# gr, za and the values of the linear-attention branch as 2x2 block products in seven multiplications

## The chip, the cores and the metric

The kernel runs on one core of a Trainium2 chip. The metric is the device time of one execution in microseconds (us). PE is TensorE (matmuls), ACT is ScalarE, DVE is VectorE, POOL is GpSimd, and SP is the engine from which most DMAs are issued.

## What is computed

One block of a hybrid network on x of 512 tokens by 1024 features, all in float32:

```python
n = rmsnorm(x, g_mix)
gq, gk, gv, gr, z_gf, z_gb, cq, ckv, kr, z_ma, z_mb = split(n @ w_in)   # 1024 x 5824
y_gla  = rmsnorm(gated_linear_attention(gq, gk, gv, z_gf, z_gb), g_gla) * silu(gr)   # 4 heads, values 256 wide
y_mla  = latent_attention(cq, ckv, kr)                                   # 8 heads, values 128 wide
merged = sigmoid(z_ma) * y_gla + sigmoid(z_mb) * y_mla
h = x + merged @ w_out
h = h + square(relu(rmsnorm(h, g_mlp) @ w_ff1)) @ w_ff2                  # 4096 wide
out = rmsnorm(h, g_final)
```

gr, za (that is z_ma) and gv are each 512 tokens by 1024 columns of `n @ w_in`, zb (z_mb) too; gq and gk are 512 by 512, 128 columns for each of the four heads of the linear attention. The scale of the first rmsnorm is one number per token, so the kernel multiplies x (times g_mix) by the weights first and puts the token's scale on the product.

## The kernel before

**Precision.** Both operands of a product are split into hi and lo parts in TensorE's float32r type. `split` (L92 to L94) writes hi on ACT as a rounded copy and lo on DVE as the difference; `split_scaled` (L96 to L98) does it with a factor. `mm3` (L87 to L90) issues three matmuls for each product: hi by hi, hi by lo, lo by hi. Most of the matmuls of the kernel stand at L88, L89 and L90 for that reason.

**Buffers.** SBUF tiles come from pools by size: `u2` (128x512, 25 buffers), `u4` (128x1024, 26), `wf` for weights that have just landed (3), `wh` and `wl` for their halves (128x1024, 4 each). PSUM has two groups of four banks, `mm` and `at`. A tile's buffer goes to a later tile when all its users are done.

**Order.** The framework (Tile) plans the order of the instructions of each engine ahead of time: by the order in which they are traced, by when they are ready in its plan, and by which buffers are free. Where the kernel writes an order out, it uses `in_program_order` (all of a stretch, for some engines) and `goes_behind` (one stretch behind another). At run time every engine works through its own queue in order.

**Stages.** In the opening (L289 to L351), x arrives transposed (features on partitions) in eight pieces, along with eight pieces of the value weights of the first 512 columns. Each piece is split, PE multiplies it at once (`values_with`, L312 to L319, 96 matmuls at L317), and x's squares are summed up to give each token's scale: `r_x` as one number per token on a partition, `R` as a 128x512 tile in which every partition holds the scales of all tokens. `z_chunk` then projects the gates and the rotary key part. After that each projection is one call of `proj_T` (L240): it loads 1024x128 weights, splits them, and PE makes a tile of 128 features by 512 tokens with 24 matmuls of 512 columns. So gr, za, zb, gq and gk have features on partitions, and the token's scale is applied with `R`. `gla_g1` (L539) makes gr's and za's gates for a head; `gla_v` (L505) makes the second half of the values with tokens on partitions.

**Heads.** For each head h of four (L800 to L861): `gla_g1`, then `gla_qk` (gq and gk projected, multiplied by the decays of `gate_parts` on DVE, scaled for neighbouring and far chunks on POOL, L450), a zb projection, `gla_scores`, a second zb projection, `gate_parts` for the next head, and `gla_out` (L556): two 128x512 tiles of features by tokens, 24 matmuls of 512 columns. Its norm over 256 features runs across partitions, so `gla_rstd` sums the squares with matmuls against ones (L255) and `gla_norm` spreads the scale over the partitions with two more (L282). Head 3 also holds the latent projections. Then come the latent attention (L864 to L880), `w_out`, and the squared-ReLU stage.

**The squared-ReLU stage.** The second of its products (`@ w_ff2`) is already done as 2x2 block products in seven multiplications (L1007 to L1090): the weights' block sums (`add_w2`, L997) and the sums of the activations (L1066 to L1069) are made on DVE, and the weights of each product are split two products ahead (`prep`).

Of the kernel before, what the change touches and what calls it, by code (L numbers as in the profile page):

```python
# [56 lines left out]
def tile_block(ctx: ExitStack, tc: tile.TileContext, t, out: bass.AP):  # L57
# [10 lines left out]
    def u2(name, dt=F32, shape=(P, S)):  # L68
        return tl(list(shape), dt, "u2", 25, name)
# [218 lines left out]

    xT = [u4(f"xT{k}") for k in range(KD)]  # L289
# [3 lines left out]
    for k in range(KD):  # L293
        nc.sync.dma_start(xraw[k], t["xt"][k * P : (k + 1) * P, :])
        nc.sync.dma_start(vraw[k], w_in[k * P : (k + 1) * P, C_GV : C_GV + S])
    load_gates()

    def v_tiles(pr):
        return [u4(f"gv{pr}{i}") for i in range(NT)]

    def v_evict(acc, hl, i):
        split_scaled(hl[:, 0, :], hl[:, 1, :], acc, r_x[:, i : i + 1])
# [5 lines left out]
    v_accs = [ps("mm", f"gv0{i}") for i in range(NT)]  # L308
    vh = [halves(2, S, f"gv0{k}") for k in range(KD // 2)]
    sq = None  # L310

    def values_with(k):  # L312
        hi, lo = xT[k][:, 0, :], xT[k][:, 1, :]
        wh, wl = vh[k // 2][0][:, k % 2, :], vh[k // 2][1][:, k % 2, :]
        for x, (a, b) in enumerate(((hi, wh), (hi, wl), (lo, wh))):
            for i in range(NT):
                nc.tensor.matmul(  # L317
                    v_accs[i], a[:, i * P : (i + 1) * P], b, start=k == 0 and x == 0, stop=k == KD - 1 and x == 2
                )  # L319
# [8 lines left out]
    for k in range(KD):  # L328
# [8 lines left out]
        if k < 6:  # L337
            values_with(k)
# [4 lines left out]
    values_with(6)  # L343
    values_with(7)
# [3 lines left out]
    v = v_tiles(0)  # L348
    for i in range(NT):
        v_evict(v_accs[i], v[i], i)  # L350
# [39 lines left out]
    def gate_parts(h):  # L390
        l = u4("l", F32)
        ms = []
        for i, d in enumerate(("f", "b")):
            bcol = (V_BF if d == "f" else V_BB) + h
            bias = gvec[:, bcol : bcol + 1]
            acc = ps("at", f"gate{d}")
# [32 lines left out]

    def gla_qk(h, parts):  # L430
# [3 lines left out]
        for x, (col, name) in enumerate(((C_GQ, "gq"), (C_GK, "gk"))):  # L434
            acc = proj_T(col + h * P, f"{name}{h}")
            n = u2(f"{name}n{h}")
            if x == 0:
                nc.vector.scalar_tensor_tensor(n, acc, GQ_SCALE, R, op0=ALU.mult, op1=ALU.mult)
            else:
                nc.vector.tensor_tensor(n, acc, R, op=ALU.mult)  # L440
            for d in ("f", "b"):
                nc.vector.tensor_tensor(  # L442
                    near[d][:, x].rearrange("p a b -> p (a b)"), n,
                    parts[d][0][:, x].rearrange("p a b -> p (a b)"), op=ALU.mult,
                )
# [59 lines left out]
    def gla_v(pr):  # L505

        accs = [ps("mm", f"gv{pr}{i}") for i in range(NT)]
        col = C_GV + pr * S
        res = v_tiles(pr)

        def piece(i, k2, wh, wl):
            tok = slice(i * P, (i + 1) * P)
            for kk in range(2):
                k = 2 * k2 + kk
                mm3(accs[i], xT[k][:, 0, tok], xT[k][:, 1, tok], wh[:, kk, :], wl[:, kk, :], k == 0, k == KD - 1)

        kept = []
        for k2 in range(KD // 2):
            wh, wl = weights(w_in[k2 * 2 * P : (k2 + 1) * 2 * P, col : col + S], f"gv{pr}{k2}")
            if k2 >= 2:  # L520
                kept.append((k2, wh, wl))
                continue
            for i in range(NT):
                piece(i, k2, wh, wl)
        for i in range(NT):
            for k2, wh, wl in kept:
                piece(i, k2, wh, wl)
            v_evict(accs[i], res[i], i)
        return res

    def gated(acc, name):

        z = u2(f"z{name}")
        nc.vector.tensor_tensor(z, acc, R, op=ALU.mult)  # L534
        th = u2(f"t{name}")
        nc.scalar.activation(th, z, AF.Tanh, scale=0.5)
        return z, th

    def gla_g1(h, js=(0, 1)):  # L539

        res = []
        for j in js:
            f = 2 * h + j
            z, th = gated(proj_T(C_GR + f * P, f"gr{f}"), f"r{f}")
            g1 = u2(f"g1{f}")
            nc.vector.scalar_tensor_tensor(g1, th, 1.0, z, op0=ALU.add, op1=ALU.mult)
            _, ta = gated(proj_T(C_ZA + f * P, f"za{f}"), f"a{f}")
            nc.vector.scalar_tensor_tensor(g1, ta, 1.0, g1, op0=ALU.add, op1=ALU.mult)
            res.append(g1)
        return res  # L550
# [5 lines left out]
    def gla_out(h, sc, v, g1, name):  # L556
        accs = [ps("at", f"{name}o{j}") for j in range(2)]
        for dv in range(2):
            for j in range(NT):
                at = (h % 2) * GDV + dv * P  # L560
                c = slice(at, at + P)
                mm3(accs[dv], v[j][:, 0, c], v[j][:, 1, c], sc[j][:, 0, :], sc[j][:, 1, :],
                    j == 0, j == NT - 1)
        sq = []
        for dv in range(2):
            s = u2(f"{name}sq{dv}")
            nc.scalar.activation(s, accs[dv], AF.Square)
            sq.append(s)
            f = 2 * h + dv
            nc.vector.scalar_tensor_tensor(  # L570
                g1[dv], accs[dv], gla_gain[:, f : f + 1], g1[dv], op0=ALU.mult, op1=ALU.mult
            )
        nc.vector.tensor_tensor(sq[0], sq[0], sq[1], op=ALU.add)
        return sq[0]

    def gla_rstd(sq, g1, name, early):

        at = traced()
        tot = feature_sums(sq, name, "mm")
        if early is not None:  # L580
            goes_behind((at, traced()), early, PE_ONLY)
        return rstd_diag(tot, GDV, name, False), g1, name

    def gla_norm(diag, g1, name):
        rs = spread(diag, name, "mm")
        for dv in range(2):
            nc.vector.tensor_tensor(g1[dv], g1[dv], rs, op=ALU.mult)
        return g1
# [205 lines left out]
    y1, g2 = [], []  # L794
    z_chunk()
    g1 = gla_g1(0, (0,))
    parts = gate_parts(0)
    g1 += gla_g1(0, (1,))
    waiting = None
    for h in range(GH):  # L800
        last = h == GH - 1
        if h:
            g1 = gla_g1(h)
        if h == GH - 2:
            cos, sin = rotary_tables()
        near, nxt, far = gla_qk(h, parts)
        if last:
# [8 lines left out]
            waiting = gla_rstd(*waiting, (marks[1], marks[2]))  # L816
            marks.append(traced())
            next(cq_steps)
            goes_behind((marks[1], marks[2]), (marks[0], marks[1]), PE_ONLY)
            goes_behind((marks[3], traced()), (marks[2], marks[3]), PE_ONLY)  # L820
            ckv = next(ckv_steps)
            y1 += gla_norm(*waiting)
            next(cq_steps)
        if h == 2:
            v = gla_v(1)
        if h == 2:
            began = traced()
            sc = gla_scores(near, nxt, far)
            waiting = gla_rstd(*waiting, (began, traced()))
            g2.append(mla_g2(2 * h))  # L830
        else:
            began = traced()
            zb = proj_T(C_ZB + 2 * h * P, f"zb{2 * h}")
            projected = traced()
            sc = gla_scores(near, nxt, far)
            scored = traced()
            goes_behind((projected, scored), (began, projected), PE_ONLY)
            if h == 1:
# [390 lines left out]
```

## Time and profile before

| what | value |
|---|---|
| time, three runs | 780.64 us median (780.55 to 781.74) |
| profiled execution | 781.0 us, of which span 779.3 us |
| granted TensorE clock, mean | 0.997 |
| busy in the span | PE 770.3 us (99%), DVE 543.8 (70%), ACT 407.1 (52%), POOL 97.8 (13%) |
| instructions | 9996, of which 3728 matmuls |
| DMA | 73.94 MB, 95 GB/s in the mean |

The span goes from the first to the last instruction of the profiled execution; the time of the same execution is 1.7 us longer. Busy shares are means over stages that differ. A matmul's busy time overlaps with the next one's, so its price is read from the distance between starts.

### The profile page before, as it was taken

To read this page: it belongs to the slowest core of one execution; us is meant where nothing else is said; L and a number is where in the kernel's file an instruction comes from. 1 tells how busy PE (TensorE), PEld (TensorE's weight loads), DVE (VectorE), ACT (ScalarE), POOL (GpSimd) and SP (SyncE) were. 2 spreads that over 40 slices of the span, in tenths; PEclk is the share of its full clock that TensorE was granted. 3 is DMA by queue.
4 is the path that set the end of the run, shared out by engine and by line. 5 is a ranking of instruction groups with operands and counts; after the bars stand their busy time and mean duration, and the time that the engine had idled before them with its cause. 6 is when DMAs were issued, how large, how long until landed. Compare 5 with 4: busy or idle time off the path is not lost.

```text
span 779.3 us, 9996 instructions
## 1 busy us (share of the span) xinstructions
PE 770.3 (99%) x3728; PEld 647.9 (83%) x3728; DVE 543.8 (70%) x833; ACT 407.1 (52%) x677; POOL 97.8 (13%) x166
## 2 busy tenths in 40 slices
PE   9999999999999999999999999999999999999996
PEld 7888888888888888898888888888888888888885
DVE  7767555765574459699963578865787578848695
ACT  7463622732462336697852466535554465436644
POOL 1023103203011213221110100000000000000014
PEclk9999999999999999999999999999999999999998
DMA  7633143243323312233033731164106411560002
GB/s 250 178 94 108 27 108 82 61 115 82 82 54 101 56 42 63 53 108 95 28 136 92 261 108 54 56 191 133 54 14 201 141 51 28 163 187 2 28 1 108
DMA packets 102401, 73.94 MB, mean 95 GB/s; under 512 B 15088, under 2 KB 86768, under 8 KB 102352
## 3 DMA queue, kind: packets, MB, share of 16 engines
q1 hardware_dynamic: 101264, 70.14, 31.5%
q10 hardware_dynamic: 864, 2.38, 0.8%
q0 software_dynamic: 224, 0.79, 0.4%
q8 instruction: 29, 0.48, 0.3%
q14 instruction: 20, 0.16, 0.1%
HBM read 69.62 MB, written 2.10 MB: 92 GB/s over the span
## 4 chain that ended last, share of the span: by engine, by line
PE 91%; issue 4%; DVE 2%; POOL 1%; ACT 0%; POOLq 0%
PE f L89 8%; PE f L90 7%; PE f L88 7%; PE gx L88 4%; PE gx L90 4%; PE gx L89 4%; PE gv L317 3%; PE wo L88 2%; PE wo L89 2%; PE gz L89 2%; PE wo L90 2%; PE gr L88 2%; PE za L88 2%; PE za L89 2%; PE gr L89 2%
## 5 line engine op out<-in xcount | busy, mean ns | idle before, releaser
L997 DVE TENSOR_TENSOR w<-w,w 128x1024 f32<-128x1024 f32 x32 | 38.7, 1219 | 0.4
L1172 POOL DMA_DIRECT2D gfin<-in_g_final x1 | 0.7, 653 | 282.7 <-PE f L90 282.7
L759 ACT ACTIVATE e<-s,top 128x512 f32<-128x512 f32 x32 | 21.9, 685 | 5.8 <-DVE top L756 5.8
L944 DVE TENSOR_TENSOR h<-gx,h 128x512 f32<-128x512 f32 x32 | 21.5, 683 | 1.9 <-PE gx L90 1.8
L94 DVE TENSOR_TENSOR pT<-tp,pT 128x512 fp32r<-128x512 f32 x32 | 21.6, 677 | 0.4 <-ACT pT L93 0.4
L756 DVE TENSOR_REDUCE top<-s 128x1 f32<-128x512 f32 x32 | 21.5, 676 | 0.0
L93 ACT ACTIVATE pT<-tp 128x512 fp32r<-128x512 f32 x32 | 18.9, 592 | 3.4 <-PE tp L773 3.3
L773 PE MATMUL tp<-ident,e 128*128 128x128 f32 x128 | 19.2, 272 | 0.0
L88 PE MATMUL av<-pT,v 128*128 128x256 f32 x64 | 19.1, 299 | 0.0
L1050 ACT ACTIVATE fa<-f 128x512 f32<-128x512 f32 x32 | 18.5, 577 | 0.0
L89 PE MATMUL av<-pT,v 128*128 128x256 f32 x64 | 18.4, 287 | 0.0
L90 PE MATMUL av<-pT,v 128*128 128x256 f32 x64 | 18.3, 286 | 0.0
L773 PEld LDWEIGHTS tp<-ident,e 128*128 128x128 f32 x128 | 15.6, 140 | 3.1
L450 POOL TENSOR_TENSOR qk<-qkf,e3f 128x256 f32<-128x256 f32 x8 | 7.9, 981 | 81.8 <-DVE qkf L442 81.8
L791 POOL TENSOR_TENSOR tb<-tb,g 128x512 f32<-128x512 f32 x8 | 11.1, 1382 | 53.1 <-DVE tb L790 40.1
L93 ACT ACTIVATE gbh<-y 128x512 fp32r<-128x512 f32 x16 | 10.1, 634 | 14.0 <-DVE y L1067 14.0
L1059 ACT ACTIVATE px<-fa 128x256 f32<-128x256 f32 x32 | 13.4, 419 | 1.0
L88 PE MATMUL s<-kbuf,q 96*128 96x512 f32 x32 | 13.8, 432 | 0.0
L534 DVE TENSOR_TENSOR za<-za,R 128x512 f32<-128x512 f32 x8 | 5.5, 689 | 11.8 <-PE za L90 11.8
L93 ACT ACTIVATE b_10h<-w 128x1024 fp32r<-128x1024 f32 x7 | 7.4, 1059 | 12.1 <-PE gz L90 6.0
L93 ACT ACTIVATE b_20h<-w 128x1024 fp32r<-128x1024 f32 x7 | 7.4, 1059 | 12.1 <-PE gz L90 6.0
L93 ACT ACTIVATE b_00h<-w 128x1024 fp32r<-128x1024 f32 x7 | 7.4, 1058 | 12.1 <-PE gz L90 6.0
(1454 smaller groups left out, 2791.8 us busy)
## 6 DMA issues: line engine op xcount, KB each, us to landing
w<-in_w_ff SPq DMA_DIRECT2D x64, 256.0 KB, 3.5
x<-in_xt SPq DMA_DIRECT2D x8, 256.0 KB, 5.2
vw<-in_w_in SPq DMA_DIRECT2D x8, 256.0 KB, 5.3
h<-in_x ACTq DMA_DIRECT2D x4, 512.0 KB, 5.2
out<-ms SPq DMA_DIRECT2D x7, 256.0 KB, 2.2
q<-ro SPq DMA_DIRECT2D x16, 64.0 KB, 2.3
gr0f<-in_w_in SPq DMA_DIRECT2D x1, 512.0 KB, 4.9
za0f<-in_w_in SPq DMA_DIRECT2D x1, 512.0 KB, 5.9
```

The costliest lines, as they stand in the source:

```text
L88: nc.tensor.matmul(acc, lh, rh, start=start, stop=False, skip_group_check=onto)
L89: nc.tensor.matmul(acc, lh, rl, start=False, stop=False, skip_group_check=onto)
L90: nc.tensor.matmul(acc, ll, rh, start=False, stop=stop, skip_group_check=onto)
L93: nc.scalar.activation(hi, src, AF.Copy)
L94: rest.tensor_tensor(lo, src, raw(hi), op=ALU.subtract)
L317: nc.tensor.matmul(v_accs[i], a[:, i * P : (i + 1) * P], b, start=k == 0 and x == 0, stop=k == KD - 1 and x == 2)
L756: nc.vector.tensor_reduce(top, acc, axis=AX.X, op=ALU.max, negate=True)
L759: nc.scalar.activation(e, acc, AF.Exp, bias=top, accum_out=tot)
L773: nc.tensor.transpose(tp[:, k * P : (k + 1) * P], e[:, k * P : (k + 1) * P], ident)
L944: nc.vector.tensor_tensor(hc, acc, hc, op=ALU.add)
L997: nc.vector.tensor_tensor(wq[dst][g], wq[x][g], wq[y][g], op=op)
L1050: nc.scalar.activation(a, acc, AF.Relu)
```

## The change

gr, za and gv (each 512 tokens by 1024 columns, over 1024 features) become block products with tokens on partitions. x is cut into four blocks (256 tokens by 512 features), the weights into four blocks (512 by 512), and seven products of blocks, of 24 matmuls each, give the four blocks of the result (Winograd's form). The block sums of x are made once on POOL (`x_sums`, `more_x_sums`) and used by all three; the differences of weight blocks are made on POOL in place (`less`). PE's order over the products, and POOL's from `x_sums` to the last of them, are written out with `in_program_order`. The opening now multiplies gq and gk of head 0 and the first two zb projections with features on partitions (weights in a gathered input, `w_first`); those projections drop out of their later places. The head outputs are made with tokens on partitions (48 matmuls of 256 columns); their norm sums along the row on ACT, the gates are multiplied on DVE, the scale on POOL, and `gla_turn` transposes the result with eight 128x128 transposes a head. The column sums and the spreading of the scale on PE drop out. `u2` has 29 buffers instead of 25, and the DMA scratch space is set to 8192.

```diff
+    def x_sums():
+        add = nc.gpsimd.tensor_tensor
+        for p in range(KD // 2):
+            a, b = xraw[p], xraw[p + KD // 2]
+            for u, k in ((a, p), (b, p + KD // 2)):
+                nc.scalar.activation(u, u, AF.Copy, scale=gmix[:, k : k + 1])
+            y = u2(f"xy{p}")
+            add(y[:, LO], a[:, HI], b[:, HI], op=ALU.add)
+            add(y[:, HI], y[:, LO], a[:, LO], op=ALU.subtract)
+            sy = u4(f"xsy{p}")
+            split(sy[:, 0], sy[:, 1], y)
...
+    class Seven:
+        def load(self, x):
+            self.blocks[x] = [u4(f"{self.name}w{x}{g}", F32, (P, 2, S)) for g in range(2)]
...
+        def less(self, dst, x, y):
+            for g in range(2):
+                nc.gpsimd.tensor_tensor(
+                    self.blocks[dst][g], self.blocks[x][g], self.blocks[y][g], op=ALU.subtract
+                )
+        def prepare(self, m):
+            x = {1: 0, 2: 2, 5: 0, 6: 0, 3: 3, 7: 1, 4: 2}[m]
+            if m == 5:
+                self.less(0, 1, 0)
+            elif m == 6:
+                self.less(0, 3, 0)
+            elif m == 3:
+                self.less(2, 2, 0)
+            elif m == 7:
+                self.less(1, 3, 1)
+            self.right[m] = []
+            for g in range(2):
+                wh, wl = halves(2, S, f"{self.name}{m}{g}")
+                split(wh, wl, self.blocks[x][g])
+                self.right[m].append((wh, wl))
+        def product(self, m):
...
+            for rb in range(2):
+                acc, tok = accs[rb], slice(rb * P, (rb + 1) * P)
+                for p in range(KD // 2):
+                    lh, ll = x_left[p][m]
+                    wh, wl = right[p // 2]
+                    mm3(acc, lh[:, tok], ll[:, tok], wh[:, p % 2, :], wl[:, p % 2, :],
+                        begin and p == 0, p == KD // 2 - 1, not begin)
+                if m in (1, 5, 6):
+                    c = {1: self.c11, 5: self.c22, 6: self.c12}[m][rb]
+                    nc.scalar.activation(c, acc, AF.Copy)
+                elif m == 4:
+                    self.sink(2 + rb, 0, acc, u2(f"{self.name}d"))
+                else:
+                    c = {2: self.c11, 3: self.c12, 7: self.c22}[m][rb]
+                    nc.vector.tensor_tensor(c, acc, c, op=ALU.add)
+                    self.sink(rb + (2 if m == 7 else 0), int(m != 2), c, c)
+    def gr_rows(i, half, src, dst):
+        th = u2(f"tr{i}{half}")
+        nc.scalar.activation(th, src, AF.Tanh, scale=r_half[:, i : i + 1])
+        nc.vector.scalar_tensor_tensor(dst, th, 1.0, src, op0=ALU.add, op1=ALU.mult)
...
     z_chunk()
-    g1 = gla_g1(0, (0,))
...
+    for x in (0, 2, 1, 3):
+        sevens[0].load(x)
+    x_sums()
+    zb_gate(2)
+    steps = [(a, m) for a in range(3) for m in SEVEN]      # order: 1, 2, 5, 6, 3, 7, 4
+    for a, m in steps[:2]: sevens[a].prepare(m)
+    for n, (a, m) in enumerate(steps):
+        if n + 2 < len(steps):
+            b, mm = steps[n + 2]
+            if a + 1 < 3:
+                for x in {3: (0,), 7: (2, 1), 4: (3,)}.get(m, ()): sevens[a + 1].load(x)
+        if m == 7:
+            sevens[a].product(m)
+            if a == 0: zb_gate(3)
+            elif a == 2: project_qk(1, 0)
+        if n + 2 < len(steps):
+            sevens[b].prepare(mm)
+            if n == 0: more_x_sums()
+        if m != 7: sevens[a].product(m)
+        if a == 2 and m == 3: parts = gate_parts(0, "mm")
+    near, nxt, far = gla_qk(0, parts)
     for h in range(GH):
...
+        sc = gla_scores(near, nxt, far)
+        if h:
+            gla_turn(h - 1, (projected, scored))
...
+            project_qk(h + 1, 1)
+            parts = gate_parts(h + 1)
+            gla_out(h, sc)
+            if h < 2: zb_gate(4 + h)
+            if h < 2: project_qk(h + 2, 0)
+            near, nxt, far = gla_qk(h + 1, parts)
```

More of the change, by code (lines that the diff above doesn't have):

```diff
@@ L433, in gla_qk @@
             near[d] = u4(f"qk{d}", F32, (P, 2, NT, P))
[L434 to L440, printed above, removed]
+        for x in range(2):
+            n = qk.pop((h, x))
             for d in ("f", "b"):
@@ L531, in gated @@
[L531 to L550, printed above, removed]
+    SEVEN = (1, 2, 5, 6, 3, 7, 4)
@@ L552, in mla_g2, with gv_rows @@
+    def gv_rows(i, half, src, dst):
+        v[i, half] = u4(f"gv{half}{i}")
+        split_scaled(v[i, half][:, 0, :], v[i, half][:, 1, :], src, r_x[:, i : i + 1])
     def mla_g2(f):
         return gated(proj_T(C_ZB + f * P, f"zb{f}"), f"b{f}")[1]
[L556 to L574 removed]
@@ new lines, in gla_turn @@
+    def gla_turn(h, early=None):
+        half, at = h // 2, (h % 2) * GDV
+        began = traced()
+        for dv in range(2):
+            f = 2 * h + dv
+            tp = ps("at", f"y1{f}")
+            for i in range(NT):
+                nc.tensor.transpose(
+                    tp[:, i * P : (i + 1) * P], g1[i, half][:, at + dv * P : at + (dv + 1) * P], ident
+                )
+            y = u2(f"y1{f}")
+            nc.scalar.activation(y, tp, AF.Copy, scale=gla_gain[:, f : f + 1])
+            y1.append(y)
+        if early is not None:
+            goes_behind((began, traced()), early, PE_ONLY)
```

236 lines of the change are left out of this document (144 added, 92 removed).

## The prediction, made before the changed kernel ran

> **What bounds the kernel now.** I read the page first (busy time, the chain that ended last), then the stretch from 29 to 300 us, in which all the projections lie, then single matmuls for their spacing, and last the vector engines, on which the change puts its new work.
>
> ```profile
> PE 770.3 (99%) x3728; PEld 647.9 (83%) x3728; DVE 543.8 (70%) x833; ACT 407.1 (52%) x677; POOL 97.8 (13%) x166
> ...
> PE 91%; issue 4%; DVE 2%; POOL 1%; ACT 0%; POOLq 0%
> ```
>
> PE is busy for 770.3 of 779.3 us, and the chain is PE for 91%. The windows say the same of the changed stretch (PE, PEld, DVE, ACT, POOL busy, then the granted clock):
>
> ```profile
> 29.00:300.00 271.00, 270.87 (x1262) 226.20 (x1262) 168.60 (x267) 122.47 (x170) 52.36 (x101) 1.00 0.31 79
> ```
>
> PE stands still for 0.13 us of 271; DVE works 62%, ACT 45%, POOL 19%. Every matmul taken away is therefore time won, as long as the others keep up. Busy time per matmul overlaps, so the price is the distance between starts, from the timeline of PE (start, duration):
>
> ```profile
> 45.16 0.39 PE L89 MATMUL gr<-xT,gr1h 128*128 128x512 f32 x1
> 45.39 0.39 PE L90 MATMUL gr<-xT,gr1l 128*128 128x512 f32 x1
> ...
> 396.96 0.28 PE L88 MATMUL av<-pT,v 128*128 128x256 f32 x1
> 397.08 0.28 PE L89 MATMUL av<-pT,v 128*128 128x256 f32 x1
> ```
>
> From 44.71 to 49.47 us lie 21 steps of 512 columns: 0.2267 us each. Steps of 256 columns take 0.119 (396.01 to 397.20, ten of them). The other prices on PE stand in the chain in order of time:
>
> ```profile
> 129.85 0.79 PE gla0ss L255 x8
> 136.70 0.46 PE gla0rs L282 x2
> 436.28 0.87 PE mb L197 x8
> ```
>
> A head's column sums cost 0.79, the spreading of its scale 0.46, eight 128x128 transposes 0.87.
>
> **PE's own sum.** Each of gr, za and values needs 8 x 8 x 3 = 192 matmuls of 512 columns now, and 7 products x 2 x 4 x 3 = 168 after: 3 x 24 x 0.2267 = 16.3 us off. The opening 96 matmuls stay 96 (gq0, gk0, zb0, zb1 instead of values) and the later projections lose just those. Head outputs: 24 x 0.2267 = 5.44 becomes 48 x 0.119 = 5.71, four times: +1.1. Transposes: 4 x 0.87 = +3.5. Column sums and spreading go: 4 x (0.79 + 0.46) = -5.0. Together -16.7 us, all of it on the path, since PE is the path.
>
> **What the rest must now do.** A product takes PE 24 x 0.2267 = 5.44 us. For it ACT and DVE split two 128x1024 blocks, and four products in seven first need two POOL subtractions of 128x1024. DVE and POOL hinder each other, as two timelines side by side show:
>
> ```profile
> 62.33 0.99 POOL L450 TENSOR_TENSOR qk<-qkf,e3f 128x256 f32<-128x256 f32 x1 [5.33 <-DVE qkf L442]
> 63.28 1.59 POOL L450 TENSOR_TENSOR qk<-qkf,c3f 128x256 f32<-128x256 f32 x1
> 64.83 0.61 POOL L450 TENSOR_TENSOR qk<-qkb,e3b 128x256 f32<-128x256 f32 x1
> 757.41 1.29 POOL L1100 TENSOR_TENSOR ms<-h,gfin 128x512 f32<-128x512 f32 x1
> ```
> ```profile
> 62.76 1.64 DVE L94 TENSOR_TENSOR gr2l<-gr2f,gr2h 128x1024 fp32r<-128x1024 f32 x1
> ...
> 757.20 0.68 DVE L944 TENSOR_TENSOR h<-gz,h 128x512 f32<-128x512 f32 x1
> 757.80 1.99 DVE L94 TENSOR_TENSOR b_31l<-w,b_31h 128x1024 fp32r<-128x1024 f32 x1
> ```
>
> The split's subtraction, two SBUF inputs, takes 1.22 us when alone (1.14 between starts). At 757.80 it takes 1.99: it ends 1.1 after POOL's 1.29 us are over. At 62.76 it waits for one POOL instruction (1.64), and POOL's next waits for it (1.59 instead of 0.61). They take turns, whole instructions at a time. The addition at 757.20 reads PSUM and SBUF and isn't lengthened. [...]
>
> POOL's price for 128x1024 is in no row. The nearest stand in its groups of instructions (last: us in all, mean ns of one) and in the answer for line 1100 (least, median and most ns):
>
> ```profile
> L94 POOL TENSOR_TENSOR wq3l<-wq3f,wq3h 128x384 fp32r<-128x384 f32 x1 | 1.0, 1016 | 0.0
> ```
> ```profile
> L1100 POOL TENSOR_TENSOR ms<-h,gfin x4: 1288/1291/2160, 757.4 to 764.1; 128x512 f32<-128x512 f32 x4
> ```
>
> 128 more columns cost 0.27 us, so 512 more cost 1.1: I take 1.29 + 1.1 = 2.4 us (between 1.2, DVE's price, and 3.3, from the 2.16 of the hindered one). [...]
>
> So in one set of seven products the shared way carries 8 x 2.4 (POOL) + 14 x 1.14 (splits) + 6 x 0.61 (sinks with two SBUF inputs) = 38.9 us against PE's 38.1. The mean almost fits; the order doesn't. Only two products' split weights fit in the four buffers, so a split can't run ahead, as the squared-ReLU stage shows on ACT, which has the same seven products with its subtractions on DVE:
>
> ```profile
> 498.34 1.06 ACT L93 ACTIVATE b_00h<-w 128x1024 fp32r<-128x1024 f32 x1 [2.93 <-PE gz L90]
> 499.70 1.06 ACT L93 ACTIVATE b_01h<-w 128x1024 fp32r<-128x1024 f32 x1 [0.30 <-PE gz L90]
> ```
>
> The hi half of product m+2 starts 1.36 us (6 matmuls) before product m ends. Between that point of product 1 and the start of product 3 lie 3 x 5.44 + 1.36 = 17.7 us (order 1, 2, 5, 6, 3). In them DVE must do 6 splits and 2 sinks (8.1 us of the shared way) and 2 additions from PSUM (1.2), while POOL works off the subtractions for 6, 3 and 7, which are due one behind the other: 6 x 2.4 = 14.4. All in turn make 23.7, 6.0 too late; with POOL's last one behind the stretch, 3.6. I take 4.5 a set, between these two, with ends of 1.2 (POOL's last two behind it) and 7.0 (the next split, too, waits part of a turn): 13.5 us, from 3.6 to 21. PE's order is written out there, so nothing else fills such a gap.
>
> **Other stalls.** *Start*: eight 512 KB blocks are queued ahead of zb2's weights; gr0 and za0 landed 1.7 us apart (21.6, 23.3), so zb2's land near 35 while PE is through with the gate projection at 32.7; x sums (16 POOL additions near 0.7, 8 splits of 0.61) fall in the same 15 us. 0 if product 1 goes first, 5 otherwise: 2.5, in the middle. *zb3*, put between 7 and 4, gets its buffers 1.36 us before its turn but needs 1.06 + 1.22: 1.5 (0.5 to 2). *gq1* in the third set has the same wait, and stands behind the decays of head 0:
>
> ```profile
> 82.30 0.67 ACT L398 ACTIVATE l<-gatef,gvec 128x512 f32<-128x512 f32 x1
> ...
> 87.55 1.28 ACT L427 ACT_TABLE_LOAD   x1
> ...
> 93.57 0.62 ACT L421 ACTIVATE eeb<-difb 128x512 f32<-128x512 f32 x1
> ```
>
> From the gate's matmul (81.3) to its last exponential (94.2) are 12.9 us, on ACT with two table loads of 1.28; DVE has scans and differences of some 4 us in it, then 4 products of 0.6 and 8 POOL multiplications of 0.61 follow: 20 us until scores can run. Ahead of gq1 or of scores, 6 us (1 to 10), the middle. *Heads 1 and 2*: between gates and scores PE now has head outputs, zb and gq, 5.7 + 2 x 5.44 = 16.6 us, against those 20: 3.4 short each, less if gk is pulled forward: 3 in all (0 to 7). SP's queue carries the blocks early (two of a set at a time, 4 to 6 us to land): no charge, and if one came late, its landing time. ACT keeps 2.1 of 5.44 us in splits and 1.2 in sinks: hidden by PE. Sum of stalls: 2.5 + 13.5 + 1.5 + 6 + 3 = 26.5 (5 to 45).
>
> **Total.** -16.7 + 26.5 = +9.8. The profiled execution took 781.0 (span 779.3, 1.7 around it), 0.36 above the median of 780.64: 790.8 for it, 790.4 for the median. About 0.2% (1.6 us) is what a measurement of this kernel can tell from no change.
>
> **Rivals.** *The cover holds* (faster): POOL's subtractions fall into times in which DVE waits for buffers (ACT's 2.93 us of idle above shows such times), so a set of products runs without a gap, as in the squared-ReLU stage, where PE is busy for 49.00 of the 49.00 us from 491 to 540. Then only some 3 us of stalls at the start and in gq1 are left: 780.6 - 16.7 + 3 = 767. It decides against me if all stalls stay under 15. For it: the means, 38.9 against 38.1, with a filler of 5.44 in two sets. Against it: there the subtractions cost DVE 1.14 and block nobody; here 2.4 and they block. Chance 0.26, and 0.04 for a draw between (stalls of 15 to 18). *The clock falls in the gaps* (slower still): the profile's opening matmuls on the identity come 0.236 us apart (16 in 3.78), those of warm PE 0.109: a cold PE is half as fast. Today's longest wait inside the stretch is under 0.5 us, so no row shows how long a gap cools it. If five gaps do, each followed by about 3.8 us at half pace: 5 x 1.9 = +9.5, 800. [...] Chance 0.18. My forecast has 0.52, its own range being 782 to 800.
>
> **Range and chances.** 767 to 804 takes in the stalls from about 3 to 40 and leaves out half of the first rival and the end of the second. Faster 0.26, same 0.04, slower 0.52 + 0.18 = 0.70.
>
> **What would show it.** Right: gaps of 2 to 3 us ahead of products 6 and 3 in each set, POOL subtractions at 2.4 to 3.6 us, splits on DVE at up to 3.5 instead of 1.22, PE's sum of matmul steps down 16 to 17 us, a longer gap at gq1 or the first scores. Wrong: PE without idle from 33 to 165 us, or POOL's subtractions well under 2 us, or DVE's splits still at 1.22; a granted clock under 1.00 would speak for the second rival.

## The result, and the profile after

The changed kernel takes 824.48 us (823.2 to 825.04), the kernel before on the same chip 781.19 (780.55 to 781.79): a ratio of 1.055, 95% interval 1.053 to 1.057. The forecast was 790.4, its range 767 to 804. So it is slower, as forecast, but by 43.3 us and not by 9.8.

The page of the changed kernel, the busy times and then the chain that ended last:

```profile
PE 772.7 (94%) x3744; PEld 646.2 (79%) x3744; DVE 605.0 (74%) x838; ACT 450.7 (55%) x761; POOL 202.6 (25%) x230
...
PE 70%; DVE 13%; ACT 6%; POOL 6%; issue 3%; DMA 0%; POOLq 0%; DVEq 0%; ACTq 0%
```

PE was the chain for 91%, now for 70%; most of the rest is work of DVE, ACT and POOL for which PE stood still. The same stretch as before, in windows (PE, PEld, DVE, ACT, POOL busy, then the granted clock):

```profile
29.00:300.00 271.00, 234.00 (x1067) 191.68 (x1066) 206.29 (x230) 142.03 (x205) 133.95 (x139) 0.94 0.23 71
```

PE is idle for 37 us where it was idle for 0.13, and the granted clock fell from 1.00 to 0.94: the work that is left also runs slower. The view of waits for PE (in all, times, longest) names the places:

```profile
PE sc L506 <- POOL qk L462: 9.8, 3, 4.4
PE grx L89 <- DVE gr60l L94: 9.8, 1, 9.8
PE ckvss L255 <- DVE ckvs L703: 3.9, 1, 3.9
PE sc L505 <- ACT bds L497: 2.8, 1, 2.8
PE bd L493 <- DVE qkb L454: 1.9, 1, 1.9
PE zaz L89 <- DVE za30l L94: 1.7, 1, 1.7
```

One wait of 9.8 us in gr's set of products, four of 1.7 us in the next two sets (the last line is one of them), and 18 us in the heads (column sums of ckv included). From the starts of the matmuls between 5 and 430 us: distances that are longer because PE waited add up to 48.3 us (1.2 before), distances that are longer because the single matmul was slow to 18.2 (5.5 before). That is 47.1 + 12.7 = 59.8 us more; the span grew by 822.6 - 779.3 = 43.3, so PE's own sum, which is what remains, is 16.5 shorter.

**The first set.** DVE, POOL and what they do to each other (timelines: start, duration):

```profile
52.41 1.21 DVE L94 TENSOR_TENSOR gr51l<-grw,gr51h 128x1024 fp32r<-128x1024 f32 x1
53.54 11.18 DVE L94 TENSOR_TENSOR xsz<-xz,xsz 128x512 fp32r<-128x512 f32 x4
64.64 0.68 DVE L620 TENSOR_TENSOR gra<-grw,gra 128x512 f32<-128x512 f32 x1
65.24 2.76 DVE L94 TENSOR_TENSOR gr60l<-grw,gr60h 128x1024 fp32r<-128x1024 f32 x1
67.93 3.38 DVE L94 TENSOR_TENSOR gr61l<-grw,gr61h 128x1024 fp32r<-128x1024 f32 x1
```
```profile
52.56 17.66 POOL L573 TENSOR_TENSOR grw<-grw,grw 128x1024 f32<-128x1024 f32 x6 [2.96 <-DVE gr50l L94]
```

Four splits of the sums of x, 2.5 us together when nothing hinders them (e1 below), fill 11.2 us, and two splits of weights take 2.8 and 3.4 instead of 1.21. Six subtractions of POOL run through without a break beside six DVE operations: each of these DVE operations, two SBUF inputs each, waits for one whole POOL instruction, however short it is itself. The addition from PSUM (L620) passes at 0.68. The answer for the line of the subtractions (least, median and most ns) has the price alone and in turns:

```profile
L573 POOL TENSOR_TENSOR grw<-grw,grw x8: 2407/2816/3373, 34.3 to 66.9; 128x1024 f32<-128x1024 f32 x8
```

**The heads.** POOL's timeline ahead of head 1's scores, which go on at 232.88 after 4.36 us:

```profile
226.93 0.61 POOL L462 TENSOR_TENSOR qk<-qkf,c3f 128x256 f32<-128x256 f32 x1
227.53 2.92 POOL L668 TENSOR_SCALAR gra<-gra,gla0ss 128x256 f32<-128x256 f32 x2
230.43 1.81 POOL L668 TENSOR_SCALAR grd<-grd,gla0ss 128x256 f32<-128x256 f32 x2
232.22 0.60 POOL L462 TENSOR_TENSOR qk<-qkb,e3b 128x256 f32<-128x256 f32 x1
```

The scalings of head 0's outputs (L668, the change moved them to POOL) stand in POOL's queue in front of the last multiplications for head 1. The same queue holds something that the change doesn't touch in its text, the load of the positions for the rotary tables. Before, it was issued at 151.3 us. Now POOL comes to it at 268.21 (timelines of POOL, DVE and ACT, in this order):

```profile
268.21 0.78 POOL L730 DMA_DIRECT2D pos_i<-in_positions  x1
```
```profile
271.80 0.43 DVE L732 CAST ang<-pos_i 128x512 f32<-128x512 int32 x1 [8.18 <-DMA pos_i<-in_positions]
```
```profile
276.39 1.28 ACT L744 ACT_TABLE_LOAD   x1 [14.21 <-DVE ang L740]
277.69 0.63 ACT L744 ACTIVATE sin<-ang 128x512 f32<-128x512 f32 x1
278.22 0.71 ACT L745 ACTIVATE cos<-turns,half_pi 128x512 f32<-128x512 f32 x1
278.83 0.57 ACT L497 ACTIVATE bds<-bd 128x512 f32<-128x512 f32 x1
```

DVE stands for 8.2 us before the positions, ACT for 14.2 before the angles, and behind the tables stands the copy (bds) for which PE waits. That wait (2.8 us, ended at 279.46) is the one ahead of the last of head 2's four score tiles; head 3's scores run from 332.25 us without a wait. The recorded expectations below call it head 3's.

**The clock.** PE's timeline behind the wait in head 1 (x2: two matmuls in the duration):

```profile
228.13 0.39 PE L505 MATMUL sc<-qkf 128*128 128x128 f32 x2
232.88 0.79 PE L506 MATMUL sc<-qk 128*128 128x128 f32 x2 [4.36 <-POOL qk L462]
233.47 1.06 PE L507 MATMUL sc<-qk 128*128 128x256 f32 x2
234.32 0.64 PE L505 MATMUL sc<-qkf 128*128 128x128 f32 x2
```

Two matmuls of 128 columns take 0.39 ahead of the wait and 0.64 behind it; matmuls of 512 columns come 0.427 us apart after such a wait instead of 0.2267, for up to 6 us. The granted clock of this stretch, third from the end of its line in the windows, is 0.50:

```profile
230.84:237.66 6.82, 4.78 (x16) 4.21 (x17) 1.88 (x4) 1.19 (x2) 2.56 (x4) 0.50 0.12 36
```

There are six such stretches between 6 and 817 us in the changed kernel, of 3.4, 6.8 or 10.2 us, 37.6 us in all, and none between 8 and 775 us in the kernel before.

### The profile page after: what moved, and what is told of

Read it like the earlier page. It is cut to its first block, busy times and chain, and to the rows that moved or that the text cites. A ratio compares the mean times of both kernels' runs of the same rounds, so it can differ in the third digit from the quotient of the medians.

```text
span 822.6 us, 10202 instructions
## 1 busy us (share of the span) xinstructions
PE 772.7 (94%) x3744; PEld 646.2 (79%) x3744; DVE 605.0 (74%) x838; ACT 450.7 (55%) x761; POOL 202.6 (25%) x230
## 4 chain that ended last, share of the span: by engine, by line
PE 70%; DVE 13%; ACT 6%; POOL 6%; issue 3%; DMA 0%; POOLq 0%; DVEq 0%; ACTq 0%
PE f L89 7%; PE f L90 7%; PE f L88 7%; PE gx L88 4%; PE gx L90 4%; PE gx L89 4%; PE first L312 2%; POOL qk L462 2%; PE wo L89 2%; PE wo L88 2%; PE gz L90 2%; PE gz L89 2%; PE wo L90 2%; PE gz L88 2%; PE tp L870 2%
## 5 line engine op out<-in xcount | busy, mean ns | idle before, releaser
L573 POOL TENSOR_TENSOR zaw<-zaw,zaw 128x1024 f32<-128x1024 f32 x8 | 22.2, 2801 | 32.8 <-DVE za10l L94 20.7
L573 POOL TENSOR_TENSOR gvw<-gvw,gvw 128x1024 f32<-128x1024 f32 x8 | 25.0, 3164 | 18.9 <-DVE gv10l L94 14.3
L573 POOL TENSOR_TENSOR grw<-grw,grw 128x1024 f32<-128x1024 f32 x8 | 23.4, 2955 | 3.2 <-DVE gr50l L94 3.0
L888 POOL TENSOR_TENSOR tb<-tb,y 128x512 f32<-128x512 f32 x8 | 11.2, 1402 | 50.3 <-DVE tb L887 36.0
L90 PE MATMUL av<-pT,v 128*128 128x256 f32 x64 | 18.2, 285 | 0.0
L506 PE MATMUL sc<-qk 128*128 128x128 f32 x32 | 8.6, 362 | 9.8 <-POOL qk L462 9.8
L93 ACT ACTIVATE sc<-sc 128x512 fp32r<-128x512 f32 x16 | 9.2, 594 | 15.5 <-DVE sc L511 15.5
L506 PEld LDWEIGHTS sc<-qk 128*128 128x128 f32 x32 | 6.8, 264 | 10.4 <-POOL qk L462 10.4
```

Of the source, the lines that this page charges most:

```text
L90: nc.tensor.matmul(acc, ll, rh, start=False, stop=stop, skip_group_check=onto)
L93: nc.scalar.activation(hi, src, AF.Copy)
L573: nc.gpsimd.tensor_tensor(self.blocks[dst][g], self.blocks[x][g], self.blocks[y][g], op=ALU.subtract)
```

## The experiments

Each is an edit of the changed kernel or of an earlier run here; ratios are to the kernel before on the same chip.

**e1: the subtractions of weight blocks on DVE.**

```diff
         def less(self, dst, x, y):
             for g in range(2):
-                nc.gpsimd.tensor_tensor(
+                nc.vector.tensor_tensor(
```

> The subtractions of weight blocks (less, 24 of 128x1024) run on DVE instead of POOL. Changed kernel 824.5 us. Theory A (DVE and POOL take turns on the same way into SBUF, so each 2.4 us subtraction on POOL holds up the splits behind which PE waits): DVE gets 24 x 1.14 = 27 us more of its own work, but no wait of turns is left; the gaps before products 6 and 3 (20 us in the three sets, and 3 us of slower clock behind them) go: about 803 us, DVE's splits back at 1.22 us. Theory B (the stalls come from the order of the queues and the four split buffers, whoever subtracts): at least half of these gaps stay: 814 us or more.

803.89 us (1.0289, 1.0271 to 1.0306), 20.6 less, as theory A has it. The waits of gv's and za's sets are gone, the 9.8 us too. The same four splits of the sums of x as above, and DVE's subtractions, in the timeline of this run:

```profile
54.21 2.49 DVE L94 TENSOR_TENSOR xsz<-xz,xsz 128x512 fp32r<-128x512 f32 x4
56.62 2.35 DVE L573 TENSOR_TENSOR grw<-grw,grw 128x1024 f32<-128x1024 f32 x2
```

2.49 us instead of 11.18. DVE does all the subtractions itself and still is done sooner than when POOL does them.

**e2: the subtractions stay on POOL, but nothing reads what they write.**

```diff
-                    self.blocks[dst][g], self.blocks[x][g], self.blocks[y][g], op=ALU.subtract
+                    tl([P, 2, S], F32, "wf", 3, "unread"), self.blocks[x][g], b, op=ALU.subtract
```

> The subtractions stay on POOL, in the same places behind the same splits, but write to a tile that nobody reads, and the products use the undifferenced blocks (so the block differences are left out of the result). This parts two halves of theory A. A1 (the turns themselves): DVE's splits still wait for POOL's instructions, so the gaps before products 6 and 3 stay within a third of 20 us: 818 to 827 us. A2 (the subtraction lies in the chain split, subtract, split, and 2.4 us is simply longer than DVE's 1.14): with nobody waiting for it the gaps go: 801 to 808 us.

822.07 us (1.0525, 1.0506 to 1.0544), with the same wait of 9.8 us at gr's product 6, and the four splits of the sums of x take 11.18 us again. The block differences are left out of the result here; another operand, `b`, for products 5 and 6 keeps POOL's start where it was. So it isn't the data of POOL that PE waits for; it is the turns that DVE has to take with it.

**e3: the second group of sums of x two products later.**

```diff
-            if n == 0:
+            if n == 2:
                 more_x_sums()
```

> The second half of the sums of x (more_x_sums: 8 additions on POOL, 4 splits) is traced two products later. In the changed kernel its four splits stand on DVE ahead of the split for product 6 and take 11.2 us for 2.4 us of work, because each waits a turn behind a POOL subtraction; PE waits 9.8 us there. If the place in DVE's queue is what turned the turns into that gap: about 8 us off, some 815 us, with a gap of 2 to 3 us left before product 6. If the sum of POOL's and DVE's work is what counts: the gap moves to product 3 and the time stays within 2 us, 822 to 826.

823.09 us (1.0537, 1.0522 to 1.0553). As the second account has it, the wait moves, and is as long (view of waits, PE):

```profile
PE grz L88 <- ACT grc L615: 7.0, 1, 7.0
PE grz L89 <- DVE gr30l L94: 3.7, 1, 3.7
```

It stands before product 3 now, and turns are the smaller part of it. POOL comes to these sums of x behind four subtractions, and ACT stands for them (timelines of POOL and ACT):

```profile
48.71 12.79 POOL L573 TENSOR_TENSOR grw<-grw,grw 128x1024 f32<-128x1024 f32 x4 [9.32 <-DVE gr50l L94]
```
```profile
63.36 0.63 ACT L93 ACTIVATE xsz<-xz 128x512 fp32r<-128x512 f32 x1 [6.08 <-POOL xz L550]
```

So moving these four gains nothing; the run doesn't tell the number of turns from the length of POOL's queue in the set.

**e4: the scalings of the head outputs on ACT.**

```diff
-            nc.gpsimd.tensor_scalar(g, g, tot[:, i : i + 1], None, op0=ALU.mult)
+            nc.scalar.activation(g, g, AF.Copy, scale=tot[:, i : i + 1])
```

> The last scaling of a head's output (four 128x256 multiplications by the norm, L668) runs on ACT instead of POOL. In the changed kernel these stand in POOL's queue ahead of the last two multiplications for the next head's scores, and PE waits 4.4 us in each of heads 1 and 2, then runs about 3.5 us at a lower clock. If that queueing is the cause: gaps of heads 1 and 2 down to about 1 us each, and most of 5 us of slow clock gone with them: about 814 us. If the chain from the gate's matmul through the decays is long enough by itself (20 us against 16.6 of cover): 3 us or less, 821 or more.

822.34 us (1.0526, 1.0511 to 1.0542), 2 us, in the range of the second account. That doesn't show its cause: the scores of heads 1 and 2 no longer wait for POOL, but PE waits for ACT, which now has the scalings, and for what comes behind them:

```profile
PE ckvss L255 <- DVE ckvs L703: 7.9, 1, 7.9
PE sc L505 <- ACT bds L497: 5.0, 2, 3.4
PE y L678 <- DVE sc L94: 2.2, 2, 2.1
```

The scalings stand in the way on whatever queue they are; this run didn't show where they don't.

**e5: with e1, the sums of x on DVE too.**

```diff
-        add = nc.gpsimd.tensor_tensor
+        add = nc.vector.tensor_tensor
```

> The subtractions of the weight blocks are on DVE as in the run before (803.9 us), and now the sums of x too (32 operations of 128x256, about 0.4 us each by DVE's own rows of that size). What is left in the first set there is 2.4 us of waiting before the second matmul of product 5, 1.7 and 0.7 before product 6, and 1.3 to 2 at zb3. Theory: this rest too is POOL and DVE taking turns; with POOL empty there it falls below 1 us in all, and with it about 1 us of matmuls at the lower clock: 799 us (797 to 801). Rival: DVE's own queue is the limit in the first set; 13 us of additions join it, and the waits before products 5 and 6 stay or move to the start: 803 to 808 us.

802.95 us (1.0296, 1.0265 to 1.0327), not to be told from e1. Waits of 2.0 and 1.8 us before product 6, for ACT's and DVE's half of its split, took the place of those before product 5: the rival's account. The equal times fit a DVE without free time there, on which these small additions cost about what their turns did.

**e6: with e1, the scalings behind the next head's multiplications, on POOL.**

```diff
             near, nxt, far = gla_qk(h + 1, parts)
+            scale()                        # the four L668 of head h
+            # and goes_behind(each of them, gla_qk's, POOL)
```

> Subtractions of the weight blocks on DVE (803.9 us), and in heads 0 to 2 the four scalings of the head outputs (L668, 3.6 to 4.6 us on POOL) put behind the multiplications by the decays of the next head (L462) in POOL's order. Theory: POOL's order is what the scores of heads 1 and 2 wait for; the waits of 1.5 + 3.7 us and of 4.5 us fall to about 1 us each, and the matmuls at the lower clock after them come back too: 794 us (791 to 797). Rival: the chain from the gates to the decays is late by itself, or the transposes of the head outputs, which stand right behind the scores, now wait for the scalings instead: 801 to 805 us.

800.27 us (1.0241, 1.0226 to 1.0257), 3.6 less than e1, between the two. PE's waits:

```profile
PE sc L505 <- ACT bds L497: 8.3, 1, 8.3
PE sc L506 <- POOL qk L462: 1.8, 2, 1.2
```

The waits for POOL on this line fell from 8.2 us (e1) to 1.8, as the theory has it; in heads 1 and 2 alone, with L507, from 8.9 to 1.9. But head 2's wait for the copy behind the rotary tables rose from 2.9 to 8.3: PE came to it 11 us sooner, and the issue of the positions only 5.8 (243.7 against 249.5 us).

**e7: matmuls that nothing reads in PE's long waits.**

```diff
+            if (a, m) == (0, 6):
+                fill(38)                   # 38 matmuls of 128x512 into a spare tile
             sevens[a].product(m)
...                                          # fill(17) in the scores of heads 1 and 2, fill(11) ahead of head 3's
```

> The changed kernel (824.5 us) with matmuls of 128x512 into a spare PSUM tile that nothing reads, put into PE's long waits: 38 (8.6 us at 0.2267) into the 10.2 us before product 6 of the first set, 17 (3.9 us) into the 4.6 and the 4.5 us in the scores of heads 1 and 2, 11 (2.5 us) into the 3.2 us before the scores of head 3. The waits themselves don't get shorter. Theory: the clock falls because PE had nothing to do; then the matmuls of 0.43 us behind these four places go (about 2 us at each), and nothing else changes: 817 us (814 to 820). Rival: the lower clock follows something else than PE's idle time (the load of the other engines, the time since a start): 823 to 827 us, with matmuls of 0.43 us as before behind the filled waits. If the filling stretched the waits, the time would be above 827 us.

823.62 us (1.0538, 1.0522 to 1.0555). The clock theory is right on the clock: behind the filled wait of head 1, PE's timeline has

```profile
229.70 4.14 PE L530 MATMUL idle<-xT 128*128 128x512 f32 x17
233.69 0.38 PE L510 MATMUL sc<-qk 128*128 128x128 f32 x2
233.90 0.60 PE L511 MATMUL sc<-qk 128*128 128x256 f32 x2
```

0.38 and 0.60 where the changed kernel has 0.64 and 1.06; the loss there falls from 2.3 us to 0.2, behind head 2's from 1.3 to 0.2. On the time it is wrong: 0.9 us instead of 7.5. In the first set, the next split (gr61l) isn't ready any sooner. Head 2's wait for bds rose from 2.8 to 8.3: bds came only 1.8 us sooner, and PE came to it with only 7 of gk's 24 matmuls done instead of all; slow matmuls follow it as before. And the fourth filling missed its place, as `fill(11)` stands in head 3's scores, where PE doesn't wait:

```profile
327.95 1.05 PE L493 MATMUL bd<-qkb 128*128 128x128 f32 x8
328.76 2.75 PE L530 MATMUL idle<-xT 128*128 128x512 f32 x11
```

PE came to head 3's scores at 327.95 us, in the changed kernel at 331.36: 3.4 us were won up to there, and these 11 matmuls took 2.5 of them back.

**e8: e1, e5 and e6 together, and the positions loaded ahead of head 0.**

```diff
+    pos_i = u2("pos_i", I32)
+    nc.gpsimd.dma_start(pos_i, t["positions"][0].partition_broadcast(P))
     for h in range(GH):
```

> Both kinds of subtractions and sums on DVE, the scalings behind the decays' multiplications, and the load of the positions (whose issue on POOL's queue stood behind the scalings of head 1, so that the tables of sine and cosine ran on ACT just before the copy that the scores of head 3 wait for) issued ahead of head 0. Theory: each wait had its own cause and the causes add up: first set -4 us, heads 1 and 2 -9, head 3 -4 with their slow matmuls, from 803.9: 787 us (783 to 791). Rival: a wait that goes lets the next one come up behind it (the transposes, the column sums of ckv, DVE's queue): 793 to 800 us. In neither case faster than the kernel before by more than a microsecond or two.

787.7 us (1.0077, 1.0058 to 1.0097): the causes add up. e5 and e6 alone had brought 0.9 and 3.6, and the positions alone bring 10.4 (e9): 14.9, where all together bring 16.2.

**e9: the positions alone**, in the changed kernel, same edit.

> The changed kernel (824.5 us) with one move: the load of the positions (L730), whose issue on POOL's queue came at 268.2 us, behind the scalings of head 1's outputs, is issued ahead of head 0. In the changed kernel DVE waited 8.2 us for it, the sine and the cosine ran on ACT at 277.7 us, and the copy of the backward scores that head 3 waits for (3.2 us, ACT bds) stood behind them. Theory: this queue is what cost head 3's 3.2 us and, through ACT's order, the 4.3 us before the column sums of ckv; with the slow matmuls behind them: 816 us (814 to 819). Rival: the other waits of the heads are later anyway, and take up what this one leaves: 822 to 825 us.

814.09 us (1.0412, 1.0393 to 1.0431), 10.4 less by the medians and 8.1 by the profiled spans, more than the theory had. The wait for bds is gone, that before the column sums of ckv is 1.0 instead of 4.0 us. The first set's long wait is 1.6 us shorter in this profiled execution (8.2), but that is no gain: product 6 goes on at 68.30 us as against 68.06. PE came to it later, because a wait of 1.94 us in product 5 was followed by half clock here. So were two waits of 0.78 us in zb3 (windows of this run):

```profile
53.36:56.78 3.42, 3.42 (x10) 2.68 (x9) 3.42 (x3) 2.72 (x5) 3.42 (x2) 0.50 0.02 5
90.91:94.32 3.41, 3.41 (x10) 2.63 (x9) 0.75 (x2) 0.00 (x0) 2.75 (x1) 0.50 0.59 154
```

The changed kernel's profiled execution has neither stretch. The profiled execution is the slowest of e9's four, with the lowest granted clock (0.979; the fastest, 812.1 us, has 0.986).

**e10: each known wait taken out, with head 0's decays and the tables moved ahead.**

```diff
+        if (a, m) == (2, 4):
+            near, nxt, far = gla_qk(0, parts)
...
-        if h == GH - 2:
+        if h == 1:
             cos, sin = rotary_tables()
```

> A kernel that keeps the seven products and takes out each wait that the runs so far have shown: the subtractions of the weight blocks on DVE, the sums of x left on POOL, the scalings and the three small operations ahead of them behind the decays' multiplications, the positions loaded ahead of head 0, the tables of sine and cosine made in head 1, and head 0's multiplications by the decays ahead of the last product of the third set. Against the run with all three moves (787.7 us): the first set's 5.3 us of waits before products 5 and 6 become about 3.3, head 0's 2.2 + 1.5 go, head 3's 2.8 go, with 2 to 3 us of slow matmuls. Theory: 778 us (775 to 781), faster than the kernel before by up to 0.6%. Rival: DVE's queue has no room for what is moved ahead (the splits of values and of weights come later), and the waits come back in heads 0 and 1: 784 to 789 us.

789.76 us (1.0111, 1.0096 to 1.0126), the rival. PE's waits in this run:

```profile
PE sc L507 <- POOL qk L462: 3.0, 2, 1.5
PE sc L505 <- ACT bds L497: 2.5, 1, 2.5
PE y L680 <- POOL gra L669: 2.1, 2, 1.6
```

Head 0's wait changed its name from bd to sc, and the tables held up head 1's copy instead of head 2's (ACT makes them from 213.06 to 215.6, the copy starts at 215.51). The work moved ahead on a full engine came back as another wait here.

**e11 and e12: work taken out of the first set, and not only moved.** The gate weights and the low-rank gate input aren't needed before the third set; their preparation goes behind gr's product 7. The three small operations ahead of the scalings go behind the multiplications too. e11 has the sums of x on DVE, e12 on POOL; both have e1, e6 and the positions early.

```diff
+                zb_gate(3)
+                z_rest(zkl)     # gates[...], kr, z4: 5 operations on DVE, 4 on ACT
```

> The run with all three moves (787.7 us), with two more: the preparation of the gate weights and of the low-rank gate input (five operations on DVE, 3.1 us, and four on ACT), which the first set doesn't need, goes behind the first set's product 7; and the three small operations ahead of the scalings go behind the decays' multiplications with them. Theory: in the first set DVE has no free time from 43 to 69 us, and what is taken from it there comes off the waits of 1.1, 2.2 and 2.1 us before products 5 and 6, with some of the 2.5 us of slow matmuls behind them; the waits of the transposes in heads 0 and 1 stay: 783 us (781 to 786). Rival: other work of DVE moves into the room, or the order of the splits turns against product 2, and the waits stay: 786 to 789 us. Not faster than the kernel before in either case by more than the measurement can tell.

> As the run beside it, with the sums of x on POOL. Theory: POOL's additions and DVE's operations take turns, so it is the slower of the two, by 1 to 2 us: 785 us (783 to 788). Rival: with DVE as full as it is, work on POOL is worth the turns: 780 to 783 us, which would be about the kernel before.

e11: 787.05 us (1.0078, 1.0066 to 1.009), in the rival's range; e12: 784.93 (1.0053, 1.0041 to 1.0065), at the theory's figure, but faster than e11 and not slower. In both, the waits before products 5 and 6 are nearly gone (e12: none over 0.3 us), and what they gave came back in head 1, where the transposes now wait 3.7 us for the scalings (1.4 us in e8). Of the two, the sums on POOL are the better, against the theory, if narrowly (783.81 to 786.58 against 784.11 to 787.86 us): with DVE full, additions of 128x256 seem to be worth their turns; subtractions of 128x1024 weren't (e1).

**e13: with e12, the transposes of heads 0 and 1 behind the projection of k.**

```diff
-        if h:
+        if last:
             gla_turn(h - 1, (projected, scored))
...
             project_qk(h + 1, 1)
+            if h:
+                gla_turn(h - 1, (at, traced()))
```

> The best run so far (784.9 us: subtractions on DVE, sums of x on POOL, scalings late, positions early, the gate preparation behind product 7), with the transposes of heads 0 and 1 put behind the next head's projection of k instead of right behind the scores. In the run before they waited 1.4 + 0.8 + 0.8 + 0.8 us for POOL's scalings in head 1, and 1.4 us of slow matmuls followed. Theory: this wait is covered by the 5.4 us of the projection and goes: 780 us (778.5 to 782), level with the kernel before. Rival: the gate matmuls and with them the next head's decays come later by as much, and the scores of heads 2 and 3 wait: 784 to 787 us.

779.48 us (777.61 to 781.8), the kernel before 781.86: 0.9969, 0.9957 to 0.9981. This version of the change is as fast as the kernel before or, by the interval, 0.2 to 0.4% faster; the slowest of its six runs is level with it. Its busy times, and the changed stretch in windows:

```profile
PE 761.9 (98%) x3744; PEld 640.8 (82%) x3744; DVE 590.7 (76%) x862; ACT 451.4 (58%) x761; POOL 139.0 (18%) x206
```
```profile
29.00:300.00 271.00, 261.68 (x1252) 218.35 (x1251) 217.18 (x302) 162.03 (x240) 86.36 (x133) 0.97 0.26 76
```

12.4 us of waits and 12.5 of slow matmuls are left from 5 to 430 us, against 1.2 and 5.5 before: 18.2 us more, about what the seven products save; the profiled execution is the slowest of the six.

**e14: with e9, matmuls that nothing reads in the waits of heads 1 and 2.**

```diff
+            if j == 1 and h in (1, 2):
+                fill((12, 19)[h - 1])
```

> The run with the positions early alone (814.1 us), with matmuls of 128x512 that nothing reads put into PE's two longest waits of the heads: 12 (2.7 us) into the 3.6 us of head 1, 19 (4.3 us) into the 5.3 us of head 2. When the waits of the changed kernel were filled, head 3's wait took up what came back; here head 3 has no wait. Theory: the 1.8 and 2.4 us of slow matmuls behind these two waits are on the path, and PE's idle time makes them: 810 us (809 to 811.5). Rival: the decays' chains of the next heads set when the scores can run, whatever PE does between, and the waits of head 2 and of the column sums of ckv grow by as much: 813 to 816 us.

812.34 us (1.0394, 1.038 to 1.0408), between the theory's range and the rival's; the intervals of e9 and e14 overlap, so the time alone doesn't decide. The profiles do for these heads: from the first wait in head 1's scores to the transposes behind the spreading of cq's scale are 329.04 - 229.85 = 99.2 us in e9 and 324.04 - 228.45 = 95.6 in e14, 3.6 less, where 1.8 + 2.4 us of slow matmuls stood behind the two waits. In this pair of profiles, where no long wait follows, the clock's loss is real time.

## Why the prediction was wrong by 34 us

- **PE's own sum** (-16.7) came in at -16.5, by difference. The mechanism, too, was as forecast: POOL and DVE take turns over whole instructions, the POOL subtraction takes 2.4 us alone (2.39 and 2.41 the least of two sets, against the estimate of 2.4) and 2.8 to 3.4 in turns, the splits up to 3.4. (The "shared way" of the forecast, "the same way into SBUF" in the expectation for e1, is the author's picture of these turns; the runs show the turns, and none shows a way as such. The sum for one set is 38.8, not 38.9.) "The cover holds" fell with that.
- **Bursts, 3 x 4.5 = 13.5**: 13.2 + 3.8 + 4.1 = 21.1. For za and gv the step was right. In the first set it failed: the shared way was summed for a set's own operations, and the sums of x were charged to the start alone. Four of their splits fall between the splits for products 5 and 6, and the sum gave each its own duration, where the trace shows a whole turn of 2.8 us. e1 shows the four at 2.5 us without turns, e2 that it is the turns.
- **Start 2.5, zb3 1.5, gq1 with head 0 6**: 1.5, 1.8 and 1.2 + 3.8. Right, but the start by luck: zb2's weights were issued at 17.2 us and landed 4.2 later, not near 35; at 34.08 PE waited for DVE (gqn), which stood behind three splits.
- **Heads 1 and 2, 3**: 4.5 and 5.0. The step compared the length of the decays' chain with PE's cover and left out what is queued on POOL: four scalings of 0.9 us and more ahead of the last multiplications. With the order changed (e6) the waits of heads 1 and 2 for POOL fall from 8.9 to 1.9, so it was the queue and not the chain.
- **No term for the positions**: 3.5 ahead of head 2's last score tile and 4.0 before ckv's column sums in head 3. This is the step that was missing. The prediction moved the scalings to POOL and didn't ask what else POOL issues: the load of the positions, 117 us later than before, with the tables on ACT and a PE wait behind it. Alone it is worth 8 to 10 us (e9).
- **The clock at nothing**: 12.7 us of slower matmuls more than before. That it was put at nothing had no row behind it. "The clock falls in the gaps" was right in kind and near in size (9.5), but wrongly set up as a rival: it comes on top of the stalls. What it costs depends on what is next: filling won 3.4 us up to head 3 where data were late again (e7), 3.6 of 4.2 where they weren't (e14). Slow matmuls stand behind each of the four longest waits here, but also behind the wait of 3.0 us for bds (2.6 us lost) and behind 2.0 + 1.4 us with 1.2 us of matmuls between in head 0 (2.4 lost). Behind the single waits of 1.9 there are none here, but in e9 there are, behind one of 2.1 (the view of waits has 2.8, 1.9 + 1.2, 1.7 and 1.94 for these).

The terms as measured: 1.5 + 21.1 + 1.8 + 5.0 + 9.5 + 7.5 + 0.8 (small ones) = 47.2 of waits, 12.7 of clock, -16.5: 43.4 us, as against 26.5 - 16.7 = 9.8. Of the 33.6 us between, the clock is 12.7, the bursts 7.6, the positions 7.5 and heads 1 and 2 6.5; the rest cancels but for 0.7. The range failed for the missing queue and for the clock as an alternative instead of an addend: without these two 824.5 would be 804.3, at its end.

The order in which it came back: subtractions on DVE 20.6, the scalings' order 3.6, positions early with the sums of x 12.6, less work in the first set 2.8, transposes later 5.4. These are differences of medians, taken on chips on which the kernel before took 780.74 to 781.86. None of these changes touches the seven products.

## What to carry to other kernels

When work moves to an engine, list everything that engine's queue issues, the DMAs too, and ask of each who waits for it now; a load that the diff doesn't mention cost 8 to 10 us here. Price work on POOL beside DVE by counting turns: every DVE operation with two SBUF inputs that fell in the time paid one whole POOL instruction here (four splits of 0.6 us each took 2.8 each), so large POOL instructions are the worst and many small DVE operations the worst hit. The stalls of PE of 2.8 to 9.8 us in the changed kernel cost their length and then 1.3 to 2.6 us of half-speed matmuls, unless the next wait swallowed them; in e9 half clock followed one of 1.9, too. One eighth of the matmuls of three projections, on an engine that was 99% busy, was won only after most such waits were gone.

## What the runs showed of the hardware that was not expected

- The turns are strict. Six POOL subtractions (17.66 us) and six DVE operations beside them alternate one for one: four DVE splits of 2.5 us in all took 11.2. The same work all on DVE was faster than on both (e1, 803.89 us against 824.48).
- After a wait PE's matmuls of 512 columns came 0.427 us apart instead of 0.2267, for 3.4 to 6 us; after the wait of 9.8 us it was no longer, 1.7 us lost. In the trace of the changed kernel the granted clock is 0.50 around or right behind each of the four waits of 3.87 to 9.79 us, for 3.4, 6.8 or 10.2 us. Of the shorter waits the one of 2.83 us and the pair of 1.86 and 1.20 in head 0 have it, too, for 6.8 us each; the nine others of 0.5 to 1.75 us between 5 and 430 us don't, and in e9 one of 1.94 us and two of 0.78 do. What decides between them no run shows.
